# Other PSUM ring for the low-rank products, later grams kept in DRAM, two filling counts changed

## The chip, the cores and the metric

The kernel runs on one core of a Trainium2 chip, as one launch. The metric is the device time of that launch in microseconds (us); the time of a kernel is the median over its runs. The numbers of one execution below come from the hardware profiler on that core. The engines are named as in the profile: PE is TensorE (matrix products), DVE is VectorE, ACT is ScalarE, POOL is GpSimd, and SP is SyncE, whose queue issues all the DMA transfers spoken of here, in order.

## The reference, cut to what matters

Two blocks run one after the other on 512 positions of width 1024. The first mixes an RWKV-7 recurrence, a short convolution, gates, a cross-attention to 256 memory rows and an MLP; the second has windowed attention with sinks and a gated spatial mixing. The change lies in the first block, in the projections and the recurrence:

```python
h = rms_norm(x, norm_mix)                    # 512 x 1024
p = h @ w_in                                 # 1024 x 5408, then a token shift on the RWKV columns
r, k, v, wd, ad, gd, cb, cc, cx, ga, gb = split(p)
log_w = -softplus(-(w0 + tanh(wd) @ w_lora_w)) - 0.5     # low-rank product, 64 -> 512
decay = exp(-exp(log_w))
a = sigmoid(a0 + ad @ w_lora_a)                          # low-rank product, 64 -> 512
g = sigmoid(gd) @ w_lora_g                               # gate product, 160 -> 512
kk = (k * k_k) / norm(k * k_k)                           # per head of 64
k = k * (1 + (a - 1) * k_a)
# per head, state S of 64 x 64, for each position t:
S = S * decay_t + (S @ -kk_t) (kk_t * a_t)^T + v_t k_t^T
y_t = S @ r_t
...
out_a = groupnorm(y) * ... * g
merged = sigmoid(ga + ..) * (out_a @ w_proj_a) + sigmoid(gb + ..) * (conv branch @ w_proj_b)
```

There are 8 heads of 64, and all arithmetic is in float32.

## The kernel before, in words

**Products.** Each large product is made of three matmuls (`mm_fm`, lines 190 to 195): both operands are split into a high and a low part, and high x high, high x low and low x high are added up in one PSUM bank. The weights come tile by tile through SP's queue (`wload`, line 185), ACT copies the high part (line 167) and DVE takes the rest (line 168). PSUM has eight banks in three rings: three `mm`, two `sc` and three `ch`. Whoever asks for a bank of a ring gets the one that was given out longest ago, and its first write waits until that one has been read out.

**Order.** The program is one straight list of instructions. A scheduler spreads it over the engines by priority, which is the order in which the code is written, and by when operands are due; each engine then runs its own list in order. A matmul that is written inside `tc.issue_after(x)` is pinned behind the instruction x on PE.

**First products.** Six column blocks of `w_in` (the `gb` gates) are multiplied while the norm of x is still being worked out (`first_mm`). Their results stay in six banks, three of `mm` and three of `ch`, until `first_scale` (line 257) multiplies them by the norm and `gate_b_act` takes the gate. For blocks 0 to 2 this stands directly behind the norm, for blocks 3 to 5 (the `ch` banks) behind `prep(0)`.

**Preparation.** `proj_in` (line 288) makes one column block of h @ w_in, and `shift` (line 293) the token shift; its last instruction, line 297, reads the bank on DVE. Behind the blocks for the low-rank inputs `wa` and `gs` comes `prep(j)` for four pairs of heads j: the projection `k`, its squares summed per head by four small matmuls (line 349), the two low-rank products (`lora_mm`, line 329), then `kk`, `AR` (queries and `kk`, scaled by the decay), `KB` (keys), `r` and `v`. `prep_tail(j - 1)` is written inside `prep(j)` behind the projection `k`; its small matmuls `rkk` are line 396. The gate product (`gw`, `gt`, line 431) stands behind all four.

**Recurrence.** The 512 positions are taken in eight chunks of 64. For each chunk `gram(n)` (lines 451 to 465) multiplies KB with AR for all heads into two `sc` banks, and DVE masks them into a tile of tag G4 (four buffers) as it evicts them. With a width of 128 it holds what the chunk needs; a 64-wide one, in a common tile, has only the part that the inverse needs. `send_blocks` (line 472) sends the 32 x 32 diagonal blocks of a gram to `md` in DRAM by four transfers. When all eight are there, `inverse` loads them with the blocks along the partitions (`M`, line 479), inverts them all at once in 31 steps on DVE (lines 487 and 489), stores the result (`zd`, line 491) and loads it back transposed (`ZT`, line 496, eight transfers). `chunk(n)` (line 506 on) then works through one chunk: transposes of KB (line 511), products with the gram (520), with the state from before (527, from chunk 1 on), with the inverse in two halves (535), an inner product (545), the new state (`state`, line 564 on DVE) and the output (573, 577).

**Filling.** Between these short dependent steps PE works on independent products: the conv branch, the other `gb` gates, `proj_b` and the `ga` gates, cut in `units` of four steps. `fill(n)` takes the next n steps, of three matmuls each; inside a chunk they are pinned behind the matmul before them. `fill_blocks(8)` places eight whole blocks behind the inverse and ahead of chunk 0. What is left at the end of the chunks follows them directly.

**What drives the stage.** It is written at the end of `fused_kernel`'s first half (line 723 on): four grams at full width, each sent and kept, four 64-wide ones, only sent, with two filling steps behind each; the inverse; the eight blocks; then the chunks, and behind chunks 0 to 3 the full gram of the chunk four further on.

Of the kernel before, what the change touches and what calls it, by code (L numbers as in the profile page):

```python
# [10 lines left out]
F32 = mybir.dt.float32  # L11
# [3 lines left out]
ALU = mybir.AluOpType  # L15
# [4 lines left out]
D = 1024  # L20
# [7 lines left out]
NFIRST = 6  # L28
# [18 lines left out]
def fused_kernel(ctx, tc, a, out):  # L47
    nc = tc.nc
    PE, V, S, G = nc.tensor, nc.vector, nc.scalar, nc.gpsimd

    cst = ctx.enter_context(tc.tile_pool(name="cst", bufs=1))
    reg = ctx.enter_context(tc.tile_pool(name="reg", bufs=1))
# [7 lines left out]
    def nm(s):  # L60
        uid[0] += 1
        return f"{s}_{uid[0]}"
# [10 lines left out]
    def tt(name, shape=(128, T), dt=F32):  # L73
        return tp.tile(list(shape), dt, tag="t", bufs=10, name=nm(name))
# [4 lines left out]
    def mmbank():  # L79
        return ps.tile([128, T], F32, tag="mm", bufs=3, name=nm("mm"))  # L80
# [4 lines left out]
    def chbank():  # L85
        return ps.tile([128, T], F32, tag="ch", bufs=3, name=nm("ch"))
# [10 lines left out]
    gmask = cst.tile([128, 128], F32, name="gmask")  # L97
# [159 lines left out]
    def first_scale(blk):  # L257
        fs[blk] = tt("fs")
        V.tensor_tensor(fs[blk], first[blk], rxs, op=ALU.mult)
# [9 lines left out]
    def gate_b_act(j, p):  # L269
        S.activation(bt[:, j], p, AF.Tanh, bias=hbg[:, 8 + j:9 + j], scale=0.5)  # L270
# [42 lines left out]
    for i in range(2):  # L313
        sg = tt("sg")
        shift(proj_in(1 + i), 13 + i, sg)
        S.activation(sg, sg, AF.Tanh, scale=0.5)
        t = gsr[:, i]
        S.activation(t[:, 0], sg, AF.Copy, bias=1.0)
        V.scalar_tensor_tensor(t[:, 1], sg, 1.0, t[:, 0].bitcast(F32), op0=ALU.add, op1=ALU.subtract)
        gs.append(t)  # L320
    VU = reg.tile([128, 8, 8, 64], F32, tag="R", bufs=7, name="VU")
    AR = reg.tile([128, 4, 8, 2, 64], F32, tag="R", bufs=7, name="AR")
    KB = reg.tile([128, 4, D], F32, tag="R", bufs=7, name="KB")
# [3 lines left out]
    bon = tp.tile([128, 8, 4], F32, tag="bon", name="bon")  # L327

    def lora_mm(j):
        ps_ = [mmbank(), mmbank()]  # L330
        js = slice(j * 128, (j + 1) * 128)
        for t, (wi, xi) in enumerate(((0, 0), (0, 1), (1, 0))):
            for p, p0 in zip(ps_, (0, 64)):
                PE.matmul(p, lhsT=lhl[p0:p0 + 64, wi, js], rhs=wa[p0:p0 + 64, xi], start=t == 0, stop=t == 2)
        return ps_
# [72 lines left out]
    tail = ()  # L408
    for j in range(4):
        tail = prep(j, tail)  # L410
        if j == 0:
            for blk in range(3, NFIRST):
                first_scale(blk)
                gate_b_act(blk, fs[blk])


    gw = []
# [7 lines left out]
        gw.append(wsplit(graw, [128, T]))  # L425
    gt = []
    for tb in range(TB):
        p = mmbank()
        ts_ = slice(tb * 128, (tb + 1) * 128)
        for i in range(2):  # L430
            PE.matmul(p, lhsT=gs[i][:, 0, ts_], rhs=gw[i][0], start=i == 0, stop=False)
            PE.matmul(p, lhsT=gs[i][:, 1, ts_], rhs=gw[i][0], start=False, stop=False)
            PE.matmul(p, lhsT=gs[i][:, 0, ts_], rhs=gw[i][1], start=False, stop=i == 1)
        g = tmp("gt", bufs=4)
        for c in range(2):
            for jp in range(2):
                S.activation(g[64 * jp:64 * jp + 64, 256 * c:256 * c + 256],
                             p[64 * c:64 * c + 64, 256 * jp:256 * jp + 256], AF.Copy, scale=0.5)
        gt.append(g)
# [8 lines left out]
    lnw, lnb = lnx[:, 0], lnx[:, 1]  # L448
    order8 = [(hp, jh, jp) for hp in range(2) for jh in range(2) for jp in range(2)]

    def gram(n, nc_=128):
        if nc_ == 128:
            t = reg.tile([128, 8, 128], F32, tag="G4", bufs=4, name=nm("gram"))
        else:
            t = tt("gram", (128, 8, nc_))
        pq = [scbank(), scbank()]
        for hd in range(8):
            j, p0 = hd // 2, 64 * (hd % 2)
            x = 2 * (j % 2) + j // 2
            PE.matmul(pq[hd % 2][:, x * nc_:(x + 1) * nc_], lhsT=KB[p0:p0 + 64, j, n * 128:(n + 1) * 128],  # L460
                      rhs=AR[p0:p0 + 64, j, n].rearrange("p q c -> p (q c)")[:, 0:nc_], start=True, stop=True)
        tv = t.rearrange("p (x q) c -> p q x c", q=2)
        for q in range(2):
            V.tensor_tensor(tv[:, q], pq[q][:, 0:4 * nc_].rearrange("p (j c) -> p j c", c=nc_),
                            gmask[:, 0:nc_].unsqueeze(1).to_broadcast([128, 4, nc_]), op=ALU.mult)
        return t


# [3 lines left out]
    def send_blocks(n, g):  # L472
        for d, jp, q0, r0 in quarters:
            nc.sync.dma_start(md[q0 + 4 * n:q0 + 4 * n + 4].rearrange("h j i -> j h i"),
                              g[r0:r0 + 32, 4 * jp:4 * jp + 4, 32 * d:32 * d + 32])
# [30 lines left out]
    def chunk(n, gr, ZT, y):  # L506
# [15 lines left out]
        if n > 0:  # L522
            for j in range(4):
                ub, jh = 64 * (1 - j % 2), j // 2
                if j == 0:
                    fill(1, last)
                last = PE.matmul(pg[ub:ub + 64, jh * 128:(jh + 1) * 128], lhsT=AR[:, j, n, 0, :],
                                 rhs=sp[:, j, :], start=False, stop=jh == 1)
        for d in range(2):
# [108 lines left out]
    def fill(n, behind=None):  # L638
        for _ in range(n):
            u, k = step  # L640
            if u == len(units):
                return
            if k == 0:
                while len(loaded) < min(u + 3, len(units)):
                    load_unit()
            tiles, k0, xs, acc, head, tail_, fin = units[u]
            if head and k == 0:
                acc[0] = mmbank()
            x = xs()[k0 + k]
            if behind is None:  # L650
                mm_fm(acc[0], loaded[u][k:k + 1], [x], start=head and k == 0, stop=tail_ and k == 3)
            else:
                with tc.issue_after(behind.ins):
                    mm_fm(acc[0], loaded[u][k:k + 1], [x], start=head and k == 0, stop=tail_ and k == 3)
            if k == 3:
                loaded[u] = None
                step[:] = [u + 1, 0]
                if tail_:
                    fin(acc[0])
            else:  # L660
                step[1] = k + 1

    def fill_blocks(n):
        while n and step[0] < len(units):
            fill(1)
            if step[1] == 0 and units[step[0] - 1][5]:
                n -= 1
# [53 lines left out]


    grams = {}
    for n in (0, 1, 2, 3):
        grams[n] = gram(n)
        send_blocks(n, grams[n])
        fill(2)
    for n in (4, 5, 6, 7):
        send_blocks(n, gram(n, 64))
        fill(2)  # L730
    zts = inverse()
    fill_blocks(8)
    ys = []
    for n in range(8):
        if n % 2 == 0:
            ys.append(tt("y"))
        chunk(n, grams[n], zts[n // 4], ys[n // 2])
        if n < 4:
            grams[n + 4] = gram(n + 4)
        if n and n % 2 == 0:  # L740
            post(n // 2 - 1, ys[n // 2 - 1])
    mem_norm()
# [631 lines left out]
```

## Time and profile before

| | |
|---|---|
| median of three runs | 1310.91 us (1310.71 to 1316.2) |
| profiled execution | 1310.88 us |
| its span in the trace | 1309.2 us |
| PE busy | 1276.4 us, 97% of the span |
| DVE, ACT, POOL busy | 61%, 41%, 12% |
| chain that ended last | PE 92%, DVE 5%, DMA 1% |
| mean granted TensorE clock | 0.993 of full speed |
| traffic of the DMA engines | 34.2% of their time, 107 GB/s at HBM |

A time that is subtracted from one of the profile is subtracted from the profiled execution's 1310.88 us. Busy PE is counted from each matmul's start to its modelled end, so short gaps inside a run of matmuls don't show as waits. An idle time stands in brackets with what released the engine, and for a wait of several semaphores that is the one that came last. The granted clock has two levels, 1.00 (2.4 GHz) and 0.50 (1.2 GHz). Times in a row are from the span's start.

### The profile page before, as it was taken

The numbers are of one execution on the slowest core, as the hardware profiler recorded it, in microseconds if no ns is written. First come the engines' busy times: TensorE is split into PE (matmuls) and PEld (weight loads), VectorE is DVE, ScalarE is ACT, GpSimd is POOL, SyncE is SP. The second block draws the span as 40 slices with busy tenths as digits, with TensorE's granted clock in tenths as the row PEclk, the third lists the DMA queues.
The fourth block names the chain that finished last, engine by engine and source line by source line (L and its number), as shares of the span: only waits on it lengthen the run. The fifth ranks groups of instructions, "written<-read, shape, count | busy, mean of one in ns | idle before, by whom it ended". The sixth has DMA issues, their size and how long they took to land.

```text
span 1309.2 us, 18318 instructions
## 1 busy us (share of the span) xinstructions
PE 1276.4 (97%) x6714; PEld 1038.4 (79%) x6714; DVE 804.4 (61%) x1487; ACT 536.7 (41%) x988; POOL 158.6 (12%) x162
## 2 busy tenths in 40 slices
PE   8999999899999999999999999999999999999997
PEld 6878777677798888888888888888878777888886
DVE  6667668467648555657735636444777657664456
ACT  6544523233344444544523324224355464333332
POOL 1112200014000010011031120210322000100003
PEclk9999999899999999999999999999999999999999
DMA  7212234212233632244634535222334223323331
GB/s 235 65 64 68 74 96 124 55 43 97 81 121 117 197 97 73 77 149 138 193 110 148 172 102 177 97 90 97 95 124 136 75 79 121 97 95 97 98 114 64
DMA packets 80666, 142.37 MB, mean 109 GB/s; under 512 B 17056, under 2 KB 17184, under 8 KB 80576
## 3 DMA queue, kind: packets, MB, share of 16 engines
q1 hardware_dynamic: 80576, 141.21, 34.2%
q8 instruction: 52, 0.85, 0.3%
q14 instruction: 38, 0.31, 0.1%
HBM read 134.62 MB, written 5.24 MB: 107 GB/s over the span
## 4 chain that ended last, share of the span: by engine, by line
PE 92%; DVE 5%; DMA 1%; issue 1%; ACT 1%; POOL 0%; SPq 0%; DVEq 0%; ACTq 0%; POOLq 0%
PE mm L193 26%; PE mm L194 25%; PE mm L195 25%; PE mm L797 1%; PE mm L795 1%; PE mm L796 1%; PE sc L460 1%; PE ch L1156 1%; PE ch L535 1%; PE ch L1121 1%; DVE wlo L168 1%; PE sc L1152 1%; PE ch L195 0%; PE ch L545 0%; PE ch L193 0%
## 5 line engine op out<-in xcount | busy, mean ns | idle before, releaser
L167 ACT CAST whi<-wraw 128x512 fp32r<-128x512 f32 x398 | 246.7, 621 | 499.6 <-PE mm L194 428.1
L168 DVE TENSOR_TENSOR wlo<-wraw,whi 128x512 fp32r<-128x512 f32 x398 | 293.2, 738 | 232.4 <-PE mm L195 126.2
L193 PE MATMUL mm<-h,whi 128*128 128x512 f32 x296 | 121.2, 410 | 3.0 <-DVE k L297 3.0
L194 PE MATMUL mm<-h,whi 128*128 128x512 f32 x296 | 117.9, 398 | 0.0
L195 PE MATMUL mm<-h,wlo 128*128 128x512 f32 x296 | 117.2, 396 | 0.0
L193 PE MATMUL mm<-x2g,whi 128*128 128x512 f32 x256 | 100.2, 391 | 0.0
L195 PE MATMUL mm<-x2g,wlo 128*128 128x512 f32 x256 | 99.7, 390 | 0.0
L194 PE MATMUL mm<-x2g,whi 128*128 128x512 f32 x256 | 99.6, 389 | 0.0
L193 PE MATMUL mm<-ff,whi 128*128 128x512 f32 x256 | 99.6, 389 | 0.0
L194 PE MATMUL mm<-ff,whi 128*128 128x512 f32 x256 | 99.6, 389 | 0.0
L195 PE MATMUL mm<-ff,wlo 128*128 128x512 f32 x256 | 99.6, 389 | 0.0
L193 PEld LDWEIGHTS mm<-h,whi 128*128 128x128 f32 x296 | 56.3, 190 | 18.2 <-DVE k L297 4.6
L826 POOL TENSOR_TENSOR gt<-gt,nsq 128x512 f32<-128x512 f32 x21 | 27.7, 1320 | 317.2 <-ACT nsq L825 309.8
L195 PEld LDWEIGHTS mm<-h,wlo 128*128 128x128 f32 x296 | 56.6, 191 | 12.0
L1020 POOL TENSOR_TENSOR X<-X,d 128x512 f32<-128x512 f32 x24 | 39.0, 1625 | 221.2 <-DVE d L1018 221.2
L194 PEld LDWEIGHTS mm<-h,whi 128*128 128x128 f32 x296 | 56.7, 191 | 10.4
L194 PE MATMUL mm<-h2a,whi 128*128 128x512 f32 x152 | 59.8, 393 | 0.5 <-DVE h2a L1043 0.5
L193 PE MATMUL mm<-h2a,whi 128*128 128x512 f32 x152 | 59.4, 393 | 0.8 <-ACT h2a L1042 0.8
L195 PE MATMUL mm<-h2a,wlo 128*128 128x512 f32 x152 | 59.7, 392 | 0.0
L193 PE MATMUL mm<-h2b,whi 128*128 128x512 f32 x152 | 59.5, 392 | 0.0
L195 PE MATMUL mm<-h2b,wlo 128*128 128x512 f32 x152 | 59.5, 392 | 0.0
L194 PE MATMUL mm<-h2b,whi 128*128 128x512 f32 x152 | 59.3, 391 | 0.0
(482 smaller groups left out, 2698.4 us busy)
## 6 DMA issues: line engine op xcount, KB each, us to landing
wraw<-in_w_in SPq DMA_DIRECT2D x162, 256.0 KB, 2.6
wraw<-in_w_up SPq DMA_DIRECT2D x64, 256.0 KB, 2.6
wraw<-in_w_down SPq DMA_DIRECT2D x64, 256.0 KB, 2.7
adaraw<-in_w_ada SPq DMA_DIRECT2D x24, 512.0 KB, 3.6
wraw<-in_w_proj_b SPq DMA_DIRECT2D x16, 256.0 KB, 2.6
wraw<-in_w_k SPq DMA_DIRECT2D x16, 256.0 KB, 2.5
wraw<-in_w_proj_a SPq DMA_DIRECT2D x16, 256.0 KB, 2.7
wraw<-in_w_v SPq DMA_DIRECT2D x16, 256.0 KB, 2.8
```

The costliest lines, as they stand in the source:

```text
L167: S.copy(hi, src)
L168: eng.tensor_tensor(lo, src, hi.bitcast(F32), op=ALU.subtract)
L193: PE.matmul(acc, lhsT=wh, rhs=xh, start=start and k == 0, stop=False)
L194: PE.matmul(acc, lhsT=wh, rhs=xl, start=False, stop=False)
L195: PE.matmul(acc, lhsT=wl, rhs=xh, start=False, stop=stop and k == n - 1)
L460: PE.matmul(pq[hd % 2][:, x * nc_:(x + 1) * nc_], lhsT=KB[p0:p0 + 64, j, n * 128:(n + 1) * 128], rhs=AR[p0:p0 + 64, j, n].rearrange("p q c ...
L535: last = PE.matmul(pu[r0:r0 + 32, hs], lhsT=ZT[r0:r0 + 32, n % 4, b, :], rhs=gh[r0:r0 + 32, d, hs], start=True, stop=True)
L795: PE.matmul(acc, lhsT=xh, rhs=wh, start=k == 0, stop=False)
L796: PE.matmul(acc, lhsT=xl, rhs=wh, start=False, stop=False)
L797: PE.matmul(acc, lhsT=xh, rhs=wl, start=False, stop=last)
L826: G.tensor_tensor(self.acc, self.acc, sq, op=ALU.add)
L1020: G.tensor_tensor(X[:, j], X[:, j], d, op=ALU.add)
```

## The change

The two low-rank products of each pair of heads and the gate product take their banks from the ring `ch`. For that the scaling of the first blocks 3 to 5, whose results sit in the three `ch` banks, moves from behind `prep(0)` into the loop over the two `gs` blocks: block 3 behind the first, 4 and 5 behind the second.

The 64-wide grams are gone. Grams 4 to 7 come first, at full width, are sent and then stored whole to `gd` in DRAM; grams 0 to 3 follow, are sent and kept in the four buffers. Behind chunks 0 to 3 the later gram is loaded from `gd` where it was computed.

The pinned filling ahead of line 527 goes from one step to two, and the filling ahead of chunk 0 from eight blocks to nine.

```diff
--- before.py
+++ after.py
@@ -318,6 +318,9 @@
         S.activation(t[:, 0], sg, AF.Copy, bias=1.0)
         V.scalar_tensor_tensor(t[:, 1], sg, 1.0, t[:, 0].bitcast(F32), op0=ALU.add, op1=ALU.subtract)
         gs.append(t)
+        for blk in range(3 + i, 4 + 2 * i):
+            first_scale(blk)
+            gate_b_act(blk, fs[blk])
     VU = reg.tile([128, 8, 8, 64], F32, tag="R", bufs=7, name="VU")
     AR = reg.tile([128, 4, 8, 2, 64], F32, tag="R", bufs=7, name="AR")
     KB = reg.tile([128, 4, D], F32, tag="R", bufs=7, name="KB")
@@ -327,7 +330,7 @@
     bon = tp.tile([128, 8, 4], F32, tag="bon", name="bon")
 
     def lora_mm(j):
-        ps_ = [mmbank(), mmbank()]
+        ps_ = [chbank(), chbank()]
         js = slice(j * 128, (j + 1) * 128)
         for t, (wi, xi) in enumerate(((0, 0), (0, 1), (1, 0))):
             for p, p0 in zip(ps_, (0, 64)):
@@ -408,10 +411,6 @@
     tail = ()
     for j in range(4):
         tail = prep(j, tail)
-        if j == 0:
-            for blk in range(3, NFIRST):
-                first_scale(blk)
-                gate_b_act(blk, fs[blk])
 
 
     gw = []
@@ -425,7 +424,7 @@
         gw.append(wsplit(graw, [128, T]))
     gt = []
     for tb in range(TB):
-        p = mmbank()
+        p = chbank()
         ts_ = slice(tb * 128, (tb + 1) * 128)
         for i in range(2):
             PE.matmul(p, lhsT=gs[i][:, 0, ts_], rhs=gw[i][0], start=i == 0, stop=False)
@@ -448,21 +447,21 @@
     lnw, lnb = lnx[:, 0], lnx[:, 1]
     order8 = [(hp, jh, jp) for hp in range(2) for jh in range(2) for jp in range(2)]
 
-    def gram(n, nc_=128):
-        if nc_ == 128:
-            t = reg.tile([128, 8, 128], F32, tag="G4", bufs=4, name=nm("gram"))
-        else:
-            t = tt("gram", (128, 8, nc_))
+    def gram_tile():
+        return reg.tile([128, 8, 128], F32, tag="G4", bufs=4, name=nm("gram"))
+
+    def gram(n):
+        t = gram_tile()
         pq = [scbank(), scbank()]
         for hd in range(8):
             j, p0 = hd // 2, 64 * (hd % 2)
             x = 2 * (j % 2) + j // 2
-            PE.matmul(pq[hd % 2][:, x * nc_:(x + 1) * nc_], lhsT=KB[p0:p0 + 64, j, n * 128:(n + 1) * 128],
-                      rhs=AR[p0:p0 + 64, j, n].rearrange("p q c -> p (q c)")[:, 0:nc_], start=True, stop=True)
+            PE.matmul(pq[hd % 2][:, x * 128:(x + 1) * 128], lhsT=KB[p0:p0 + 64, j, n * 128:(n + 1) * 128],
+                      rhs=AR[p0:p0 + 64, j, n].rearrange("p q c -> p (q c)"), start=True, stop=True)
         tv = t.rearrange("p (x q) c -> p q x c", q=2)
         for q in range(2):
-            V.tensor_tensor(tv[:, q], pq[q][:, 0:4 * nc_].rearrange("p (j c) -> p j c", c=nc_),
-                            gmask[:, 0:nc_].unsqueeze(1).to_broadcast([128, 4, nc_]), op=ALU.mult)
+            V.tensor_tensor(tv[:, q], pq[q].rearrange("p (j c) -> p j c", c=128),
+                            gmask.unsqueeze(1).to_broadcast([128, 4, 128]), op=ALU.mult)
         return t
 
 
@@ -523,7 +522,7 @@
             for j in range(4):
                 ub, jh = 64 * (1 - j % 2), j // 2
                 if j == 0:
-                    fill(1, last)
+                    fill(2, last)
                 last = PE.matmul(pg[ub:ub + 64, jh * 128:(jh + 1) * 128], lhsT=AR[:, j, n, 0, :],
                                  rhs=sp[:, j, :], start=False, stop=jh == 1)
         for d in range(2):
@@ -721,22 +720,23 @@
 
 
     grams = {}
-    for n in (0, 1, 2, 3):
+    gd = dr.tile([4, 128, D], F32, tag="gd", bufs=1, name="gd")
+    for n in (4, 5, 6, 7, 0, 1, 2, 3):
         grams[n] = gram(n)
         send_blocks(n, grams[n])
-        fill(2)
-    for n in (4, 5, 6, 7):
-        send_blocks(n, gram(n, 64))
+        if n > 3:
+            nc.sync.dma_start(gd[n - 4], grams[n].rearrange("p h c -> p (h c)"))
         fill(2)
     zts = inverse()
-    fill_blocks(8)
+    fill_blocks(9)
     ys = []
     for n in range(8):
         if n % 2 == 0:
             ys.append(tt("y"))
         chunk(n, grams[n], zts[n // 4], ys[n // 2])
         if n < 4:
-            grams[n + 4] = gram(n + 4)
+            grams[n + 4] = gram_tile()
+            nc.sync.dma_start(grams[n + 4].rearrange("p h c -> p (h c)"), gd[n])
         if n and n % 2 == 0:
             post(n // 2 - 1, ys[n // 2 - 1])
     mem_norm()
```

The lists below show two engines. A name with a number is one tile, and its numbers differ between the two kernels; a count at the end stands for that many equal instructions in a row. In the changed kernel the lines behind the new scaling loop carry other numbers: line 473 is `send_blocks`, 478 the load of `M`, 490 `zd`, 495 `ZT`, 611 `gmem`, 728 the store to `gd`, 739 the load from it, and 510, 519 and 534 are the transposes, the gram products and the inverse's products of a chunk.

SP's queue in the gram stage, up to the load of `M`; `gram` are the grams, `wraw` the weight tiles of the filling. Before:

```order
L474 DMA md<-gram_1519 32x4x32 x4
L185 DMA wraw_1859<-in_w_in 128x512
L474 DMA md<-gram_1542 32x4x32 x4
L474 DMA md<-gram_1571 32x4x32 x4
L474 DMA md<-gram_1596 32x4x32 x4
L185 DMA wraw_1878<-in_w_in 128x512
L474 DMA md<-gram_1626 32x4x32 x4
L474 DMA md<-gram_1649 32x4x32 x4
L474 DMA md<-gram_1678 32x4x32 x4
L185 DMA wraw_1898<-in_w_in 128x512
L185 DMA wraw_1917<-in_w_in 128x512
L479 DMA M<-md 128x1024
```

And in the changed kernel:

```order
L473 DMA md<-gram_1478 32x4x32 x4
L728 DMA gd<-gram_1478 128x1024
...
L473 DMA md<-gram_1601 32x4x32 x4
L473 DMA md<-gram_1631 32x4x32 x4
L185 DMA wraw_1864<-in_w_in 128x512
L473 DMA md<-gram_1654 32x4x32 x4
L185 DMA wraw_1883<-in_w_in 128x512
L473 DMA md<-gram_1683 32x4x32 x4
L185 DMA wraw_1903<-in_w_in 128x512
L185 DMA wraw_1922<-in_w_in 128x512
L185 DMA wraw_1947<-in_w_in 128x512
L478 DMA M<-md 128x1024
```

The first four sends are now followed by a store each, the first weight load comes behind the fifth send where it came behind the second, and three weight loads stand directly ahead of `M` where there were two.

SP's queue at the inverse's end; `zd` and `ZT` are its result on the way to DRAM and back, `gmem` the norm weights of the memory rows. Before:

```order
L185 DMA wraw_2327<-in_w_in 128x512
L491 DMA zd<-Z 128x1024
L185 DMA wraw_2367<-in_w_in 128x512
L612 DMA gmem<-in_norm_mem 128x1024
L496 DMA ZT_1808<-zd 32x16x32 x4
L496 DMA ZT_1813<-zd 32x16x32 x4
```

And in the changed kernel:

```order
L185 DMA wraw_2251<-in_w_in 128x512
L611 DMA gmem<-in_norm_mem 128x1024
L490 DMA zd<-Z 128x1024
L185 DMA wraw_2327<-in_w_in 128x512
L185 DMA wraw_2361<-in_w_in 128x512
L495 DMA ZT_1813<-zd 32x16x32 x4
L495 DMA ZT_1818<-zd 32x16x32 x4
L185 DMA wraw_2399<-in_w_proj_b 128x512
L739 DMA gram_2307<-gd 128x1024
```

`gmem` has moved from between `zd` and `ZT` to ahead of `zd`, a second weight load stands between these two, and the first load from `gd` follows two places behind `ZT`.

PE's list at the start of chunk 0; `mm` is a bank of the filling, `sc` and `ch` banks of the chunk. Before:

```order
L511 MATMUL sc_2145<-ident,KB 128x128 x4
L520 MATMUL ch_2152<-VU,gram_1477 64x64 x8
L193 MATMUL mm_2170<-h_42_385,whi_2107 128x512
L194 MATMUL mm_2170<-h_42_385,whi_2107 128x512
L195 MATMUL mm_2170<-h_42_385,wlo_2108 128x512
L193 MATMUL mm_2170<-h_42_385,whi_2107 128x512
L194 MATMUL mm_2170<-h_42_385,whi_2107 128x512
L195 MATMUL mm_2170<-h_42_385,wlo_2108 128x512
L460 MATMUL sc_2263<-AR,KB 128x128 x4
L460 MATMUL sc_2264<-AR,KB 128x128
L535 MATMUL ch_2153<-gh_2154,ZT_1808 32x64 x8
```

And in the changed kernel:

```order
L510 MATMUL sc_2194<-ident,KB 128x128 x4
L519 MATMUL ch_2201<-VU,gram_1601 64x64 x8
L193 MATMUL mm_2219<-h_42_385,whi_2151 128x512
L194 MATMUL mm_2219<-h_42_385,whi_2151 128x512
L195 MATMUL mm_2219<-h_42_385,wlo_2152 128x512
L193 MATMUL mm_2219<-h_42_385,whi_2151 128x512
L194 MATMUL mm_2219<-h_42_385,whi_2151 128x512
L195 MATMUL mm_2219<-h_42_385,wlo_2152 128x512
L510 MATMUL sc_2309<-ident,KB 128x128 x4
L510 MATMUL sc_2444<-ident,KB 128x128 x3
L534 MATMUL ch_2202<-gh_2203,ZT_1813 32x64 x8
```

Five matmuls of the gram of chunk 4 stood between the filling and the first use of `ZT`; seven transposes that belong to the next chunks stand there now.

## Rows read from the trace of the kernel before

**Rows 1.** The page: busy time, share of the span and instructions of each engine.

```profile
PE 1276.4 (97%) x6714; PEld 1038.4 (79%) x6714; DVE 804.4 (61%) x1487; ACT 536.7 (41%) x988; POOL 158.6 (12%) x162
```

**Rows 2.** Waits of PE: its line, what it waited for: us in total, times, longest.

```profile
PE ch L535 <- DMA ZT<-zd: 3.8, 1, 3.8
PE mm L193 <- DVE k L297: 3.0, 2, 1.9
...
PE sc L511 <- DVE gram L464: 1.7, 3, 0.9
...
PE mm L431 <- DVE vs L297: 0.9, 1, 0.9
...
PE ch L527 <- DVE state L564: 0.8, 1, 0.8
```

**Rows 3.** Windows: length; PE, PEld, DVE, ACT, POOL busy (x); PEclk, DMA, GB/s.

```profile
92.40:99.20 6.80, 6.80 (x20) 5.54 (x20) 3.92 (x15) 1.31 (x2) 0.00 (x0) 0.50 0.00 1
228.90:235.70 6.80, 4.67 (x34) 3.43 (x36) 0.88 (x2) 0.98 (x2) 0.00 (x0) 0.50 0.65 109
```

**Rows 4.** Timeline of PE at j=1: start, duration, instruction, [idle before <- releaser].

```profile
86.74 0.95 PE L396 MATMUL sc<-hsel,rkk 128*128 128x2 f32 x8
...
92.04 1.38 PE L349 MATMUL sc<-hsel,sq 128*128 128x2 f32 x8
...
100.13 0.47 PE L193 MATMUL mm<-h,whi 128*128 128x512 f32 x1
```

**Rows 5.** Timeline of PE at j=2, the same piece.

```profile
112.50 0.95 PE L396 MATMUL sc<-hsel,rkk 128*128 128x2 f32 x8
...
115.96 1.05 PE L349 MATMUL sc<-hsel,sq 128*128 128x2 f32 x8
...
121.20 0.48 PE L193 MATMUL mm<-h,whi 128*128 128x512 f32 x1
```

**Rows 6.** Timeline of PE, the gram stage: a wide gram and a narrow one.

```profile
166.75 1.16 PE L460 MATMUL sc<-AR,KB 64*128 64x128 f32 x16
...
169.42 1.11 PE L460 MATMUL sc<-AR,KB 64*128 64x64 f32 x16
```

**Rows 7.** Timeline of PE from the last gram to chunk 0's first use of ZT.

```profile
178.34 0.50 PE L193 MATMUL mm<-h,whi 128*128 128x512 f32 x1
...
223.38 0.60 PE L511 MATMUL sc<-ident,KB 128*128 128x128 f32 x4
...
231.03 1.27 PE L535 MATMUL ch<-gh,ZT 32*32 32x64 f32 x16 [3.75 <-DMA ZT<-zd]
```

**Rows 8.** Timelines of SP and DVE; DMA issues (KB each, median us to landing).

```profile
173.97 6.99 SPq L474 DMA_DIRECT2D md<-gram  x12
...
222.95 0.33 SPq L491 DMA_DIRECT2D zd<-Z  x1
...
188.33 0.19 DVE L487 TENSOR_TENSOR zt<-M,Z 128x31 f32<-128x31 f32 x1 [1.55 <-DMA M<-md]
...
M<-md SPq DMA_DIRECT2D x1, 512.0 KB, 6.1
zd<-Z SPq DMA_DIRECT2D x1, 512.0 KB, 3.7
```

**Rows 9.** Timeline of PE: first line 535 of chunks 1, 4, 6 and 7.

```profile
246.58 0.64 PE L535 MATMUL ch<-gh,ZT 32*32 32x64 f32 x16
...
289.77 0.64 PE L535 MATMUL ch<-gh,ZT 32*32 32x64 f32 x16
...
315.73 0.64 PE L535 MATMUL ch<-gh,ZT 32*32 32x64 f32 x16
327.95 0.64 PE L535 MATMUL ch<-gh,ZT 32*32 32x64 f32 x16
```

**Rows 10.** Instructions of line 564: count, duration ns min/median/max, first and last start.

```profile
L564 DVE TENSOR_TENSOR state<-s,PC x14: 408/744/1175, 242.4 to 324.3; 64x256 f32<-64x256 f32 x14
```

**Rows 11.** Instructions of line 464, the evictions of the grams.

```profile
L464 DVE TENSOR_TENSOR gram<-sc,gmask x24: 412/680/692, 158.4 to 286.6; 128x512 f32<-128x512 f32 x16, 128x256 f32<-128x256 f32 x8
```

## Prediction

> **What bounds the kernel now.** I read the page first: TensorE (PE) is busy for 1276.4 of 1309.2 us [rows 1], so time is won only where PE works less, stands still, or is slowed. Next the list of what PE waited for [rows 2]. All the waits that the change can touch lie in the first 340 us: 3.8 us for ZT, the transposed inverse blocks coming back from DRAM; 3.0 us at line 193 for VectorE's (DVE) `k`, in two pieces, the longer 1.9; 0.9 at the gate product (line 431) for `vs`; 1.7 for `gram` evictions; 0.8 for `state`. Third, the granted clock by stretch [rows 3]: it reads 0.50 (the 1.2 GHz level) from 92.4 to 99.2 and from 228.9 to 235.7 us, right behind the 1.9 us wait and inside the ZT wait; elsewhere around them it is full. Fourth, the timeline around these places [rows 4 to 9]. The profiled execution took 1310.88 us (span 1309.2 and 1.7 around it), the median of the runs shown 1310.91; I subtract from 1310.88.
>
> **Low-rank products in the other ring.** Before, `lora_mm` takes two of the three `mm` banks and the last projection holds the third, so the next one waits until DVE has read `k`. With `ch` banks that dependence is gone. The `ch` banks must be free of the first blocks 3 to 5 for it, which is why their scaling moves ahead.
> - j=1: from the `rkk` products (line 396) to the sums of squares (line 349) PE needs 92.04 − 86.74 = 5.30 us [rows 4]; the same piece at j=2, where nothing waits, takes 115.96 − 112.50 = 3.46 [rows 5]. Gain 1.84.
> - The clock: from line 349 to the first matmul after line 370 it takes 100.13 − 92.04 = 8.09 us at the lower level [rows 4] and 121.20 − 115.96 = 5.24 at the full one [rows 5], with equal work. Gain 2.85, if the drop goes with the wait.
> - j=0: the shorter piece is 3.0 − 1.9 = 1.1 us [rows 2]. PE only runs on to line 349, two fill matmuls later in the order than before, and there needs the square of the same `k`. Between 0 and 1.1; I take 0.5, the middle.
> - Gate product: the 0.9 us [rows 2] came from a bank held by `vs`. In the `ch` ring the fourth product waits for the first one's four copies instead, which are done by then. Gain 0.9.
> - The three scalings and gates only move from behind prep 0 to the gs loop, onto engines that wait there for PE: nothing. Uncovered they would cost a few tenths each.
>
> Sum 1.84 + 2.85 + 0.5 + 0.9 = 6.1 us.
>
> **Grams kept in DRAM.** The four later grams were computed twice, 64 wide for the inverse and 128 wide inside chunks 0 to 3. The second computation goes. The chunk starts show its price with all it causes [rows 9]: the three periods from 246.58 to 289.77 hold a gram each and sum to 43.19 us; the three from 289.77 to 327.95 hold none and sum to 38.18. Gain 5.0, between 3.5 (three times the 1.16 us of the product alone [rows 6]) and 6.5 (against the fastest period, 327.95 − 315.73 = 12.22). The gram between chunks 0 and 1 adds 1.16 and the `state` wait of 0.8 behind it [rows 2], which the second pinned step covers (three matmuls more in front of line 527): 1.9. The wider early form costs 1.16 − 1.11 per gram [rows 6], 0.2 for four. Sum 5.0 + 1.9 − 0.2 = 6.7 us. The added steps themselves cost nothing: they are taken from the filling behind the chunks.
>
> Two things could eat into it. The loads of `gd` are issued at each chunk's end and wanted three chunks later, some 38 us [rows 9], against 6.1 for the slowest such transfer to count on (`M`, [rows 8]): nothing. The state chain loses the 1.16 us of gram that stood between its producer and line 527 and gains one step, 3 x 0.23 = 0.68 us. The two state multiplications of a chunk take 0.41 to 1.18 us each, median 0.74 [rows 10], so up to 2 x (1.18 − 0.74) = 0.9 more than usual; the only wait this made before was one of 0.8. The Trainium skill (SBUF — State Buffer, section SBUF: two separate sides) says that a VectorE instruction with two SBUF inputs and a GpSimd instruction that reads SBUF exclude each other, the loser standing still for the whole instruction. By the spread of [rows 10] the trace agrees; by the rule the lengthening could come in every chunk that meets the norm's GpSimd work, by the waits seen it hardly reaches PE.
>
> **One more block of filling ahead of the chunks.** PE reaches chunk 0 at 223.38 us, after 198 fill matmuls from 178.34 on, 0.2275 us each [rows 7]. The ninth block puts 24 more in front: 5.5 us. Then PE does transposes, products and six fills before line 535, where it needs ZT: 231.03 − 3.75 − 223.38 = 3.9 us before; less five gram matmuls (0.7), plus three transposes (0.4), 3.6 after. So PE is ready at 223.4 + 5.5 + 0.2 + 3.6 = 232.7, on the clock of before.
> ZT itself gets later. SyncE's queue (SP) issues in order: twelve `md` sends took 6.99 us [rows 8], 2.3 per gram, and each of the first four grams now adds a store of some 0.4, so a gram costs SP 2.7 us, as much as its period on PE (169.42 − 166.75 = 2.67 [rows 6]); the weight loads have gathered behind them, three stand ahead of `M` instead of two, and the last evictions take 0.68 us where they took 0.41 [rows 11]. I put `M` 2 us later (bounds 0 and 3). The inverse on DVE is a chain of 222.95 − 188.33 = 34.6 us [rows 8] and stays. The store `zd` now stands behind the 512 KB load of `gmem`, which used to stand between `zd` and ZT: from nothing (the same bytes before ZT) to 6.1 − 3.7 = 2.4 us (the slower landing of a 512 KB transfer with others ahead of it); I take 0.9, nearer to nothing since the bytes only change places. ZT lands at 231.0 + 2 + 0.9 = 233.9, and 1.2 us of the 3.75 remain (bounds 0 and all 3.75). Gain 2.5. The lower clock after the wait held from 231.03 to 235.7 [rows 3, 7], 4.7 us at half speed: 2.3 more if it goes with the longer wait. Sum 4.8 us.
>
> **The sum.** 6.1 + 6.7 + 4.8 = 17.6 us: 1310.88 − 17.6 = 1293.3 us. Nothing after 340 us changes, and PE is bound there, so the gain reaches the end.
>
> **Rivals.**
> - The ZT wait stays. For it: SP has no slack in the gram stage, `M` and `zd` both have more ahead of them. Against: 5.5 us of cover for an estimated 2.9 of delay. The 1.2 us become up to 3.75 and the lower clock comes back: 1293.3 + 2.5 + 2.3 = 1298.1, at half of the wait 1296.8.
> - The lower clock is not tied to these waits. For: it falls with a wait of 1.9 us and not with one of 1.1 [rows 2, 3], so little decides. One place with a drop costs 2.85: 1296.2. The Trainium skill (TensorE: Matmul & The Clock Gate, section What's actually happening) says that the activity monitor runs freely against the kernel's start, so that the number of slow matmuls varies from run to run. By that rule drops may show up at j=0, 2 or 3 as well; in this one trace only two places have one.
> - The gram was cover, and its removal uncovers the state chain: 0.9 us in each of seven chunks, 6 us: 1299.3. For: the spread in [rows 10]. Against: the three chunks without a gram are the fastest and had three fill matmuls where there will be six.
> - Slower than before: the stores hold the gram buffers. There are four (tag G4). Grams 4 to 7 fill them, so the eviction of gram 0 waits until gram 4's sends and store have been read out, and PE waits for the `sc` bank. From the store's issue to that eviction there are four periods of 2.67 less the 2.7 us of sends and store and the 1.4 of two evictions [rows 11], 6.6 us. `zd`, the only 512 KB store to DRAM here, lands in 3.7, `M` in 6.1 [rows 8]: inside. Each microsecond beyond 6.6 costs PE four. The gain of 17.6 is gone at a landing of 6.6 + 4.4 = 11.0 us; at 12.8 it would be 1318. Nothing in the trace takes that long, but no row shows such stores among the many small sends.
>
> **Chances.** The forecast 0.55, by itself 1290 to 1296. ZT wait stays 0.25, clock elsewhere 0.10, state chain 0.06, buffers held 0.04. The best ends (6.5 for the three grams, 1.1 at j=0, no ZT wait) give 1293.3 − 1.5 − 0.6 − 1.2 = 1290.0, and a little under for the small gaps at each change of work; the first two rivals together give 1301. Range 1288.5 to 1301. Half a per cent, 6.6 us, is about what a measurement can tell from no change here: faster means under 1304.3, which the forecast and the first three rivals reach almost wholly: 0.91; same 0.05; slower 0.04.
>
> **What would show it.** Right: no line 193 wait for `k`, line 349 within 3.6 us of line 396 at j=1, the clock at 1.00 around 92 us; no line 460 after the gram stage and chunk periods of 12.7 + 0.7 us; a ZT wait at line 535 under 2 us with the clock full behind it. Wrong: a wait of line 460 for an eviction that itself waited for a DMA, line 527 waiting for `state` in several chunks, `M` landing more than 4 us after its old place beside the gram stage, or 0.50 in any window of the first 350 us.

## The result

The changed kernel takes 1299.34 us (median of six runs, 1297.71 to 1303.94) against 1310.81 of the kernel before: ratio 0.9909, 95% interval 0.9892 to 0.9926, so between 9.7 and 14.2 us faster. The forecast was 1293.3, the range 1288.5 to 1301. The sign and the range hold; 6 us of the 17.6 forecast are missing. The profiled execution took 1299.91 us, its span 1298.2.

The waits of PE in the changed kernel (line, what it waited for: us in total, times, longest):

```profile
PE ch L544 <- DVE VU L538: 6.2, 3, 2.3
...
PE ch L534 <- DMA ZT<-zd: 0.3, 1, 0.3
PE ch L526 <- DVE state L563: 0.3, 1, 0.3
```

Set against [rows 2], the waits for `k`, for `vs` and for `gram` are gone, that for ZT fell from 3.8 to 0.3, that for the state from 0.8 to 0.3. One has grown to the top of what the change can touch: 6.2 us at line 544, the inner product between the two halves of a chunk, for DVE's copy of `VU` (line 538). No step of the prediction spoke of it; in the kernel before, with other line numbers, it was small:

```profile
PE ch L545 <- DVE VU L539: 0.7, 1, 0.7
```

The windows (PE, PEld, DVE, ACT, POOL busy; then PEclk, DMA share, GB/s) answer to [rows 3]:

```profile
88.00:96.00 8.00, 7.98 (x48) 6.14 (x48) 5.23 (x19) 3.86 (x7) 0.00 (x0) 1.00 0.25 72
226.00:236.00 10.00, 9.66 (x125) 7.25 (x123) 4.16 (x8) 3.41 (x9) 0.39 (x1) 1.00 0.45 82
271.00:274.50 3.50, 3.50 (x24) 2.37 (x21) 0.55 (x2) 0.99 (x2) 0.00 (x0) 0.51 0.27 75
301.75:305.25 3.50, 3.50 (x23) 2.35 (x23) 1.10 (x2) 0.62 (x1) 0.00 (x0) 0.51 0.26 80
```

Both old drops of the clock went with their waits. Two new ones stand behind the two longest of these waits, 2.34 us each: 3.5 us each at half speed, 1.7 us lost each.

PE's timeline in chunk 3, the kernel before and then the changed one:

```profile
275.19 0.64 PE L535 MATMUL ch<-gh,ZT 32*32 32x64 f32 x16
277.44 1.02 PE L545 MATMUL ch<-VU,gram 32*32 32x64 f32 x16
279.98 0.64 PE L535 MATMUL ch<-gh,ZT 32*32 32x64 f32 x16
```

```profile
265.28 0.64 PE L534 MATMUL ch<-gh,ZT 32*32 32x64 f32 x16
269.84 0.29 PE L544 MATMUL ch<-VU,gram 32*32 32x64 f32 x2 [2.34 <-DVE VU L538]
270.07 0.55 PE L510 MATMUL sc<-ident,KB 128*128 128x128 f32 x3
270.54 0.63 PE L544 MATMUL ch<-VU,gram 32*32 32x64 f32 x14
...
273.96 0.86 PE L534 MATMUL ch<-gh,ZT 32*32 32x64 f32 x16
```

From a chunk's first use of ZT to its second PE does 12 filling matmuls and one set of line 544; this takes 4.29 us in chunks 2, 4 and 6 of the changed kernel, where nothing is late. In chunks 3, 5 and 7 it takes 8.68, 8.24 and 7.52. The excess over 4.29 in these three chunks is 11.6 us; in the kernel before it was 2.1 (4.79, 5.58 and 4.61). It measures the lateness of the copy, idle time and lower clock together, and the experiments are read by it. It is not quite clean: in chunks 3 and 5 of the changed kernel PE's list has three transposes between the two marks (0.47 us each time, above), in chunk 7 the eight matmuls of line 572 (the output), and the end of chunk 5's stretch at half speed lies behind its second mark. A longer stretch, from the first use of ZT in chunk 1 to the second in chunk 7, checks it; in the changed kernel this is 333.08 − 240.14 = 92.94 us:

```profile
240.14 0.64 PE L534 MATMUL ch<-gh,ZT 32*32 32x64 f32 x16
...
333.08 0.64 PE L534 MATMUL ch<-gh,ZT 32*32 32x64 f32 x16
```

DVE's timeline around that copy shows why it is late, the kernel before and then the changed one:

```profile
276.24 0.69 DVE L602 TENSOR_TENSOR y<-y,rq_y 128x512 f32<-128x512 f32 x1
276.96 0.42 DVE L539 COPY VU<-ch 32x256 f32<-32x256 f32 x1
278.36 0.69 DVE L604 TENSOR_TENSOR y<-y,bv 128x512 f32<-128x512 f32 x1 [0.98 <-POOL y L603]
```

```profile
266.51 0.69 DVE L601 TENSOR_TENSOR y<-y,rq_y 128x512 f32<-128x512 f32 x1
267.12 0.68 DVE L698 SCALAR_TENSOR_TENSOR bt<-bt,mm 128x512 f32<-128x512 f32 x1
268.64 0.69 DVE L603 TENSOR_TENSOR y<-y,bv 128x512 f32<-128x512 f32 x1 [0.84 <-POOL y L602]
269.37 0.42 DVE L538 COPY VU<-ch 32x256 f32<-32x256 f32 x1
```

Behind chunks 2, 4 and 6 stands `post`, the norm of the chunks just finished: eighteen DVE instructions, with one product on GpSimd (`y` times `lnw`) between line 601 and line 603. In the kernel before, the copy of the next chunk stood ahead of the addition that waits for GpSimd; now it stands behind it, and behind an eviction of the filling (line 698) too. The products that it copies were done at 265.28 + 0.64 = 265.92, so it is 3.45 us late. DVE's timeline has the same order in chunks 5 and 7, where in chunk 7 an instruction of the memory rows' norm (line 621) stands in the eviction's place. The prediction went by the lists of PE and SP alone.

### The profile page after: what moved, and what is told of

Its sections match the earlier page's. It is cut to its first block, busy times and chain, and to the rows that moved or that the text cites. A ratio compares the mean times of both kernels' runs of the same rounds, so it can differ in the third digit from the quotient of the medians.

```text
span 1298.2 us, 18193 instructions
## 1 busy us (share of the span) xinstructions
PE 1269.0 (98%) x6650; PEld 1032.9 (80%) x6650; DVE 799.5 (62%) x1479; ACT 536.1 (41%) x988; POOL 160.9 (12%) x162
## 4 chain that ended last, share of the span: by engine, by line
PE 89%; DVE 6%; DMA 2%; issue 1%; POOL 1%; ACT 0%; SPq 0%; DVEq 0%; ACTq 0%; POOLq 0%
PE mm L193 25%; PE mm L194 24%; PE mm L195 24%; PE mm L797 1%; PE mm L796 1%; PE mm L795 1%; DVE wlo L168 1%; PE sc L459 1%; DVE zt L486 1%; PE ch L1156 1%; DVE Z L488 1%; PE ch L534 1%; PE ch L1121 1%; DVE state L563 1%; PE sc L1152 1%
## 5 line engine op out<-in xcount | busy, mean ns | idle before, releaser
L193 PE MATMUL mm<-h,whi 128*128 128x512 f32 x296 | 120.2, 406 | 0.0
L194 PE MATMUL mm<-h,whi 128*128 128x512 f32 x296 | 115.9, 391 | 0.0
L195 PEld LDWEIGHTS mm<-h,wlo 128*128 128x128 f32 x296 | 55.6, 188 | 11.8
```

The costliest lines, as they stand in the source:

```text
L193: PE.matmul(acc, lhsT=wh, rhs=xh, start=start and k == 0, stop=False)
L194: PE.matmul(acc, lhsT=wh, rhs=xl, start=False, stop=False)
L195: PE.matmul(acc, lhsT=wl, rhs=xh, start=False, stop=stop and k == n - 1)
```

## The experiments

Times are medians of four to twelve runs, ratios are to runs of the kernel before beside them, with a 95% interval. "Excess" is the sum over chunks 1 to 7 of the distance just described less 4.29 us, from each kernel's trace: 2.8 before, 11.6 in the changed kernel.

**The ring alone.** The kernel before with `chbank()` in `lora_mm` and the gate product, and the scalings moved.

> The kernel before with the ring change alone (low-rank and gate products in the ch banks, scalings of blocks 3 to 5 moved). Theory A (the terms of the prediction hold for this part): 1310.8 - 6.1 = 1304.7 us by the prediction, or 6.6 less by the stretch from the first product with h to the first gram in the two traces (112.89 before, 106.25 after): 1304.2; no wait of line 193 for k, no 0.50 clock near 90 us, the ZT wait of 3.75 us unchanged. Rival B (what is won here only brings PE earlier to the ZT wait, which lengthens): the inverse moves with the grams, so B would need the ZT wait to grow to 6 us or more and the time to stay at 1309 or above.

1305.74 us, ratio 0.9965 (0.995 to 0.998): 5.1 us by the medians. The waits for `k` and `vs` and the drop near 90 us are gone; the ZT wait fell:

```profile
PE ch L534 <- DMA ZT<-zd: 2.4, 1, 2.4
```

Theory A is right on the mechanism and close in size; rival B is out. That the ZT wait would stay at 3.75 us was wrong: it lost 1.3 us.

**The grams alone.** The kernel before with the grams in DRAM, `fill(1, last)` and `fill_blocks(8)`.

> The kernel before with the later grams kept in DRAM alone (no ring change, one pinned step, eight blocks). Theory A (the terms of the prediction hold for this part, and without the ninth block its price at ZT shows): four grams less in the chunks, 5.0 + 1.16 - 0.2 = 6.0 us won; ZT lands later by the sends and stores, the wait at its first use grows from 3.75 to about 7 us (between the ring kernel and the changed kernel with eight blocks it went from 2.44 to 5.3 + 0.5), 3.4 lost: 1310.8 - 2.6 = 1308.2 us. Rival B (the later grams filled gaps in the chunks that are empty without them): the chunk starts keep their distance of 14 us in chunks 1 to 4, and with the later ZT the time is 1313 or more.

1308.04 us, ratio 0.9974 (0.9959 to 0.9988). The ZT wait grew to 5.8, and the first use of ZT comes every 11.5 to 13.8 us from chunk 1 to chunk 4 where it was 13.6 to 15.1:

```profile
PE ch L535 <- DMA ZT<-zd: 5.8, 2, 5.3
...
PE ch L545 <- DVE VU L539: 1.3, 2, 0.7
```

Theory A holds, to 0.2 us in the time; the wait was 1.2 us shorter than expected. With one pinned step the copies are hardly late (excess 2.8), so the grams are not what moved them.

**Eight blocks of filling.** The changed kernel:

```diff
-    fill_blocks(9)
+    fill_blocks(8)
```

> The changed kernel with eight blocks of filling ahead of chunk 0 instead of nine. Theory A (ZT's landing is set by the grams, M and the inverse and not by the filling): PE is ready 5.5 us earlier and waits for ZT 0.3 + 5.5 = 5.8 us, the 5.5 us of filling are done behind the chunks, and the lower clock behind the wait costs 2.3 more: 1299.3 + 7.8 = 1307 us, or 1305 if the clock stays. Rival B (the ninth block's weight loads and their splits stand in the way of the inverse and of zd): ZT lands earlier by 2 us or more, the wait is under 4 us and the time under 1304.

1305.66 us, 6.3 more than with nine. PE waits 5.8 us for ZT, and the clock is low for some 7 us from 224 on. Theory A holds: ZT is not earlier for the missing block. The excess stayed, at 10.0.

**One pinned step.** The changed kernel:

```diff
-                    fill(2, last)
+                    fill(1, last)
                 last = PE.matmul(pg[ub:ub + 64, jh * 128:(jh + 1) * 128], lhsT=AR[:, j, n, 0, :],
```

> The changed kernel with one pinned step ahead of the state products instead of two. Theory A (in the changed kernel PE loses 2.34 + 2.34 + 1.55 us in chunks 3, 5 and 7 because the second pinned step has put DVE's copy of VU behind the norm's addition, which waits for a GpSimd product): the copy stands ahead of that addition again, those 6.2 us go and with them the lower clock behind two of them (0.83 over 10 us twice, 3.4 us), while the state waits the step covered come back, up to 0.9 us in each of seven chunks: between 1289.7 and 1296 us. Rival B (with the grams gone DVE has too much work in these chunks and bounds them, wherever the copy stands): the waits of 1.5 to 2.3 us stay in chunks 3, 5 and 7, for VU or for the state, and the time is 1299 +- 1.5.

1293.39 us, 6 us faster than the changed kernel and ratio 0.9867 (0.985 to 0.9883) to the kernel before. Excess 3.8; the drops of the clock are gone; the state is late again:

```profile
PE ch L544 <- DVE VU L538: 1.7, 3, 0.7
PE ch L526 <- DVE state L563: 1.4, 2, 0.9
```

Theory A holds: in chunk 3 the copy stands at 265.40 us, ahead of lines 601 and 603. So the second pinned step, costed at nothing in the prediction, is what shifted the copy in the list.

**One step in chunks 3, 5 and 7 only.** The changed kernel:

```diff
-                    fill(2, last)
+                    fill(1 if n in (3, 5, 7) else 2, last)
```

> The changed kernel with one pinned step in chunks 3, 5 and 7 and two in the others. Theory A (the place of the VU copy behind the norm's addition in these three chunks is what costs): the waits for VU in chunks 3, 5 and 7 go, nothing else changes, 1299.3 - 6.2 - 3.4 = 1289.7 us, 1293 if the lower clock had other causes. Rival B (DVE bounds these chunks): 1299 +- 1.5, with the waits at the state products or at the second half instead.

1290.68 us, 8.7 less than the changed kernel, ratio 0.9851 (0.9834 to 0.9868). Excess 3.0, no low clock between 50 and 345 us, and DVE's copy in chunk 3 is ahead of the addition again:

```profile
265.35 0.69 DVE L601 TENSOR_TENSOR y<-y,rq_y 128x512 f32<-128x512 f32 x1
266.07 0.42 DVE L538 COPY VU<-ch 32x256 f32<-32x256 f32 x1
267.48 0.69 DVE L603 TENSOR_TENSOR y<-y,bv 128x512 f32<-128x512 f32 x1 [0.99 <-POOL y L602]
```

Theory A holds. The gain is 1 us short of its forecast; the excess left in these three chunks, 2.96 us, is more than that.

**The norm written later.** The changed kernel, two pinned steps everywhere:

```diff
-        if n and n % 2 == 0:
+        if n > 1 and n % 2 == 1:
             post(n // 2 - 1, ys[n // 2 - 1])
```

> The changed kernel, two pinned steps everywhere, with the call of the norm (post) written behind chunks 3, 5 and 7 instead of 2, 4 and 6, so that its work on DVE has a lower priority than the copies of these chunks. Theory A (what costs is the place of the VU copy behind the norm on DVE): the waits for VU in chunks 3, 5 and 7 go though the pinned steps stay, 1289.7 to 1292 us; the norm now meets chunks 4 and 6, whose first copy stands ahead of its last steps, for waits under 1 us. Rival B (the second pinned step itself costs, for its matmuls lengthen the chunk): 1297 or more.

1290.74 us, ratio 0.9842 (0.9813 to 0.9871). In chunk 3 the two uses of ZT are now 4.29 us apart, in chunk 4, which the norm meets, 5.58:

```profile
264.08 0.64 PE L534 MATMUL ch<-gh,ZT 32*32 32x64 f32 x16
268.37 0.64 PE L534 MATMUL ch<-gh,ZT 32*32 32x64 f32 x16
277.01 0.64 PE L534 MATMUL ch<-gh,ZT 32*32 32x64 f32 x16
282.59 0.64 PE L534 MATMUL ch<-gh,ZT 32*32 32x64 f32 x16
```

Theory A holds, though of the two waits left, 0.8 and 1.1 us, the longer is a little over what it allowed: the pinned steps do no harm by themselves, only by the place that the copy then gets.

**The norm's product on DVE.** The changed kernel:

```diff
-        G.tensor_tensor(y, y, lnw, op=ALU.mult)
+        V.tensor_tensor(y, y, lnw, op=ALU.mult)
```

> The changed kernel with the norm's product with lnw on DVE instead of GpSimd; the VU copy still stands behind the norm's last steps. Theory A (the copy is late because of all the norm work ahead of it on DVE, 11 us of it from the state on, and the wait for GpSimd is only 0.84 of that): the product costs DVE 0.68 where it waited for GpSimd, the waits for VU stay at 2.34 less 0.1 to 0.3, time 1298 to 1299.5 us. Rival B (the round trip to GpSimd is what the copy waits for): the waits fall under 1 us and the time to 1293 or less.

1293.26 us, ratio 0.9859 (0.983 to 0.9888). Neither theory holds as written: the waits fell to 3.6 us in total, the excess to 8.0, and one of the two drops of the clock went. Theory A's time is outside the interval (1289 to 1297 us), the rival's 1293 is missed by 0.3, but its waits under 1 us did not come.

```profile
263.36 0.64 PE L534 MATMUL ch<-gh,ZT 32*32 32x64 f32 x16
267.72 0.29 PE L544 MATMUL ch<-VU,gram 32*32 32x64 f32 x2 [1.70 <-DVE VU L538]
...
271.24 1.06 PE L534 MATMUL ch<-gh,ZT 32*32 32x64 f32 x16
```

So the round trip to GpSimd was worth more than theory A gave it and less than the rival did. By the excess it is 3.5 of the 11.6 us; by the longer stretch, 88.20 us here, 4.7; by the medians 6.1, with an interval too wide to tell these apart. The rest, about a half or more, remains with no GpSimd step left between the norm's last DVE instructions, and goes with the DVE work ahead of the copy.

**Both copies on ACT.** The changed kernel:

```diff
-                (V.tensor_copy, S.copy)[jp](VU[r0:r0 + 32, n, 4 * jp:4 * jp + 4, :],
+                S.copy(VU[r0:r0 + 32, n, 4 * jp:4 * jp + 4, :],
```

> The changed kernel with both VU copies of each half on ACT instead of one on DVE and one on ACT. Theory A (DVE's queue ahead of the copy is what costs): the waits in chunks 3, 5 and 7 go. The two copies take 2 x 0.36 one behind the other, as before 0.43 and 0.36; weight casts of 0.62 us ahead of them on ACT can cost up to that in some halves: 1289.7 to 1293 us. Rival B (VU copies are late for another reason than DVE's queue, as the second half of the products or ACT's own work): waits of 1.5 us or more stay at the product behind the copy, 1297 or more.

1287.56 us, ratio 0.9819 (0.9789 to 0.9848), the fastest kernel here: 11.8 less than the changed kernel, whose excess was 11.6. The excess is 0.0, the longer stretch 319.64 − 238.53 = 81.11 us, 11.8 less than in the changed kernel, and chunk 3 is even:

```profile
263.65 0.64 PE L534 MATMUL ch<-gh,ZT 32*32 32x64 f32 x16
265.80 0.64 PE L544 MATMUL ch<-VU,gram 32*32 32x64 f32 x16
267.94 0.64 PE L534 MATMUL ch<-gh,ZT 32*32 32x64 f32 x16
```

```profile
260.00:310.00 50.00, 50.00 (x555) 36.58 (x557) 31.93 (x64) 20.94 (x47) 16.60 (x15) 1.00 0.34 105
```

In the window from 260 to 310 us PE is busy throughout and the clock stays full. DVE's norm is unchanged here, GpSimd's product and the wait for it (0.86 us) included; nothing on PE waits for it any more. That shows the copy's place in DVE's queue as the cause.

**Both copies on ACT, one pinned step.** The kernel just described, with `fill(1, last)`.

> Both VU copies on ACT as in the run before it, and one pinned step ahead of the state products instead of two. Theory A (the pinned step covers the way from the state's products over DVE to line 526, and without it PE waits there): waits for the state of 0.5 to 0.9 us in several of the seven chunks, 1289 to 1292 us against 1287.6 with two. Rival B (with two copies less on DVE the state comes early enough, and the step buys nothing): no wait for the state over 0.4 us, 1287.6 +- 1.

1288.84 us, ratio 0.9831 (0.9807 to 0.9855). One wait of 0.6 us for the state is left. Against 1287.56 with two steps the medians are 1.3 us apart, which the intervals can't tell from nothing. The theories stay undecided; once DVE has no copies to do, the second step neither costs nor buys much.

**The kernel before with both copies on ACT.**

> The kernel before with both VU copies of each half on ACT. Theory A (the distance from the first to the second use of ZT in a chunk, 4.29 us where nothing is late, shows what the copy costs; over chunks 1 to 7 the kernel before has 2.8 us more than seven times that): 1310.8 - 2.8 = 1308 us. Rival B (copies on ACT gain 10 us and more in any kernel, whatever the order on DVE): 1301 or less. Rival C (in the kernel before, the gram's eviction on DVE is late next and takes the gain back): 1310.8 +- 1.

1307.33 us, ratio 0.9973 (0.9958 to 0.9988), 3.1 us by the medians; its excess fell from 2.8 to 0.1. Theory A holds: the excess measures what late copies cost in this kernel too, and the wait for `gram` rose only from 1.7 to 2.0.

## Why the prediction came out as it did

**The ring (6.1).** Right; timed alone it gained 5.1 us. From the first product with `h` to the first gram the kernel before takes 157.24 − 44.35 = 112.89 us, the changed one 152.02 − 45.77 = 106.25: 6.6 gained. Lines 399 and 352 at j=1, which answer to [rows 4], are 3.34 us apart, with the clock at 1.00:

```profile
87.54 0.95 PE L399 MATMUL sc<-hsel,rkk 128*128 128x2 f32 x8
...
90.88 1.05 PE L352 MATMUL sc<-hsel,sq 128*128 128x2 f32 x8
```

The same traces start 1.4 us apart (44.35 and 45.77), ahead of anything that the change touches: over all twelve traces this start lies anywhere from 43.9 to 45.8 us, so that part of the profiled run's time is not the change's. The term's 2.85 us for the clock went by one execution. Behind the same 1.9 us wait for `k` the clock was low for 6.8 us there and for 3.4 us in the trace of the kernel before with both copies on ACT.

**The block and ZT (4.8).** Right in its direction and near in size, with steps off both ways. SP's timeline in the kernel before and in the changed one, and then in the changed one the first step of the inverse on DVE and the first use of ZT that had to wait on PE:

```profile
182.14 0.33 SPq L479 DMA_DIRECT2D M<-md  x1
...
226.67 4.82 SPq L496 DMA_DIRECT2D ZT<-zd  x8
```

```profile
167.26 0.43 SPq L728 DMA_DIRECT2D gd<-gram  x1
...
179.36 0.33 SPq L478 DMA_DIRECT2D M<-md  x1
...
218.38 0.33 SPq L611 DMA_DIRECT2D gmem<-in_norm_mem  x1
218.80 0.38 SPq L490 DMA_DIRECT2D zd<-Z  x1
...
225.10 4.74 SPq L495 DMA_DIRECT2D ZT<-zd  x8
```

```profile
184.51 0.19 DVE L486 TENSOR_TENSOR zt<-M,Z 128x31 f32<-128x31 f32 x1 [1.99 <-DMA M<-md]
```

```profile
227.93 0.63 PE L534 MATMUL ch<-gh,ZT 32*32 32x64 f32 x14 [0.34 <-DMA ZT<-zd]
```

A store costs SP 0.43 us (forecast 0.4). From the first gram to the issue of `M` it is 182.14 − 157.24 = 24.90 us before and 179.36 − 152.02 = 27.34 now, 2.4 later (forecast 2). `M` then was in use 5.15 us after its issue instead of 6.19. The chain on DVE took 218.80 − 184.51 = 34.3 (34.6 before). From `zd` to ZT's first issue it is 6.30 us behind `gmem` instead of 3.72, 2.6 later, where I took 0.9 and had 2.4 as the upper end; ZT itself then was usable 2.83 us after its issue instead of 4.36. Together ZT came 2.1 us later, measured from the first gram (forecast 2.9), PE waited 0.3 us for it instead of the 1.2 forecast, and the clock stayed up. So the wait gave back 3.4 us instead of 2.5, of which 1.3 came with the ring alone.

**The grams (6.7).** The mechanism is right: line 459 is gone from the chunks, `gd` lands in 3.0 us, less than half of the 6.6 at which the buffers would have held PE, and no load of it is waited for. With the late copies out of the way (both copies on ACT) chunks 1 to 4 start 12.2 to 12.9 us apart with the second pinned step in, against 13.6 to 15.1 before. These three periods sum to 38.0 us against 43.19, so 5.2 less where 5.0 was forecast, though each holds three filling matmuls more and some transposes stand elsewhere; the term was not measured cleanly by itself.

**What failed** is the sentence that "the added steps themselves cost nothing: they are taken from the filling behind the chunks". Their matmuls cost nothing. But with three more matmuls ahead of line 526 the scheduler put the copy behind the norm's addition in DVE's list: the lists with one step and with two differ so, and the runs with one step have the small excess. That the scheduler does so because it reckons the products of line 534 to be ready later fits its rule but was not tested by itself. The excess in chunks 3, 5 and 7 rose by 11.6 − 2.1 = 9.5 us. Taking the step away in just these chunks lowered it by 8.6 (to 2.96) and the time by 8.7. Without the late copies the forecast would have been too cautious: with no late copy at all the kernel is at 1287.56, 23 us below the kernel before, of which 2.8 are the excess that the kernel before had.

So the time fell inside the range although a cost of some 9 us was not in the sum, and by the prediction's own signs it was right in part only. The waits at line 193 and at ZT, the piece at j=1 and the missing line 460 came out as said. But the first uses of ZT in chunks 3 and 4, and in 5 and 6, are 17.2 us apart instead of 12.7 ± 0.7, and the clock is at 0.50 in two windows of the first 350 us, which is one of the signs for wrong.

**The rivals.** The state chain's 1299.3 us matches the time by luck: PE waited 0.3 us in all for the state, and with both copies on ACT it waited 0.4 and the time was 1287.56. The buffers never held. The ZT wait did not stay. The lower clock was tied to the waits: where a wait went, the drop went, in each experiment, up to 345 us.

## What to carry to other kernels

An added instruction on a full engine can cost nothing there and much elsewhere, when a scheduler orders the other engines by its own estimate of readiness: compare the lists of every engine that hands something to the bounding one, around each hand-over, before costing an edit at nothing. A short copy on the way between two steps of the bounding engine should not share an in-order queue with a long side chain that waits for a third engine; moving it to an engine with free slots was worth more here (11.8 us) than tuning the order (8.7). A distance between two marks that is constant when nothing is late shows the price of lateness, idle time and lower clock together, where the list of waits shows only the first (11.6 against 6.2 us here); look first whether other work has come to stand between the marks.

## What the runs showed of the hardware

Between 50 and 345 us, each of PE's waits of 2.3 us and more in the middle of the work (2.34 twice in the changed kernel, 2.44, 2.36, 3.0, 3.75 and 5.3 twice in others) came with a stretch at the 1.2 GHz level, and none of 1.1 us or less did by itself. Those between went both ways: 1.55 and 1.62 us without, 1.54 and 1.70 with, and 1.9 at `k` with in three kernels. Later in the kernel it is as mixed: the 1.9 us wait at line 1176 (1175 and 1177 in others) came with such a stretch in three of the twelve traces, and a wait of 1.0 us at line 1121 in one, that with eight blocks. So for waits of 1 to 2 us the length alone does not say whether the clock falls. The windows of the changed kernel show what one costs: 2.34 us of idle and 3.5 at half speed, 4.1 together.

A 512 KB store took 3.0 us to land in the gram stage, among many small sends, and 6.3 where another transfer of 512 KB was issued 0.4 us ahead of it; the same store took 3.7 in the kernel before [rows 8], where that transfer came behind it:

```profile
gd<-gram SPq DMA_DIRECT2D x4, 512.0 KB, 3.0
...
zd<-Z SPq DMA_DIRECT2D x1, 512.0 KB, 6.3
```

Those are DMA issues of the changed kernel (KB each, median us from issue to landing). In its chunk 3 an eight-wide DVE instruction took 1.14 us where its equals take 0.17; it ended at 264.87, and the GpSimd instruction that began ahead of it ended at 264.85:

```profile
263.73 1.14 DVE L152 TENSOR_TENSOR rq_t<-rq_y 128x8 f32<-128x8 f32 x1
264.90 0.17 DVE L153 SCALAR_TENSOR_TENSOR rq_t<-rq_t,rq_v 128x8 f32<-128x8 f32 x1
```

```profile
263.54 1.31 POOL L591 TENSOR_TENSOR bv<-bv,lnx 128x512 f32<-128x512 f32 x1
```

The Trainium skill (SBUF — State Buffer, section SBUF: two separate sides) has the rule for this: a VectorE instruction with two SBUF inputs and a GpSimd instruction that reads SBUF lock each other out for a whole instruction. The trace agrees. Such a lock made the norm longer, ahead of the copy; with the copies on ACT it is still there (1.14 us again) and costs PE nothing. The kernel before has a stretched instruction at the same place of the norm too (line 150, 1.28 us), so this is not what moved the copy.
